# A gated attention/SSM block on one Trainium2 core: the output projection in Strassen's seven products per pair of token tiles, and the SSM gate computed ahead and kept in DRAM

## The chip, the cores and the metric

The kernel runs on one core of a Trainium2 chip. The metric is device time in microseconds (us). TensorE (PE) multiplies matrices, VectorE (DVE), ScalarE (ACT) and GpSimd (POOL) do the element-wise work, SyncE (SP) only issues DMA transfers; ACT issues some too. Each engine works through its own list of instructions in a fixed order and waits where it must: an instruction that waits holds up all that stand behind it on that engine.

## The reference

The sequence has L = 1024 tokens of width D = 1024, one layer, all float32.

```
h = rms_norm(x, norm_gain)
q,k,v,z_a,u,z_s,g_a,g_s = split(h @ w_in)
y_a = (band_attention(q,k,v) * silu(z_a)) @ w_attn_out
y_s = gelu(s5_ssm(u));  a,b = split(y_s @ w_glu + b_glu)
y_s = ((a * sigmoid(b)) * silu(z_s)) @ w_ssm_out
merged = sigmoid(g_a + bias_a) * y_a + sigmoid(g_s + bias_s) * y_s
out = rms_norm(x + merged @ w_out, final_gain)
```

`merged` and `w_out` are both 1024 x 1024.

## The kernel before

PE holds a 128 x 128 block of one operand as weights and streams up to 512 columns of the other past it. Every float32 product is made of three matmuls (`mm3`, lines 104 to 106): an operand is split into a rounded part `hi` (ACT, `split_hi`, line 98) and a remainder `lo` (DVE, `split_lo`, line 101), and hi*hi, hi*lo and lo*hi are added up in a PSUM bank.

Work up to the end of attention (about 463 us) is the same before and after, but for where two pools of tiles lie. What follows is a `Stream` of tasks, one after the other on PE. While a task runs, the weights of the next one are loaded (SP) and, half way through, split (ACT, DVE). Two kinds of tasks matter here:

- projection tasks (`proj_task`): 128 columns of `h @ w_in`, 2 halves x 8 x 3 = 48 matmuls, reading `hT` (the normed input, transposed, in the pool `h16`);
- output tasks (`o_task`): 128 rows of a product with 512 inner columns, 2 halves x 4 x 3 = 24 matmuls.

The order is: the last three g_a projections (`ga[NGA:]`), eight attention output tasks (`a_task`, whose evacuation multiplies by sigmoid(g_a) into the tiles `mg`), the g_s projection 0, eight GLU tasks, the g_s projection 1, and then in turn the SSM output task m (`gs[m][1]`) and the g_s projection m + 2. Here sigmoid(g_s) stays in a tile `sg` until the SSM output task of the same rows needs it. The GLU input is read back from DRAM into tiles `yr` and split into `g_hi` and `g_lo` between the attention output tasks and the GLU tasks. `w_out` is loaded by `load_wo` (512 KB a time, tile `wo_raw`) and split during the last tasks.

The last section (lines 1201 to 1246) takes eight tiles of 128 tokens. For each: load the residual row `x` (512 KB), split the 128 columns of the eight `mg` tiles into `mh` and `ml`, then 2 halves x 8 x 3 matmuls of 512 columns; the last token tile takes its second half as two of 256. `add_x` adds PSUM to `x` (DVE), ACT squares and sums, POOL multiplies by the final gain, and after the second half a chain of small instructions (`rsqrt`) gives 1/rms. The scaled row goes to a tile of its own, `o`, and from there to DRAM: the first half by ACT's queue, the second by SP's. There are two `x` tiles and two `o` tiles, so the next `x` load waits only for a DVE and an ACT instruction.

Of the kernel before, what the change touches and what calls it, by code (L numbers as in the profile page):

```python
# [45 lines left out]
def trunk_kernel(ctx: ExitStack, tc: tile.TileContext, x, x_t, ng, w_m, w_v, bias, a_re, a_im, log_dt,  # L46
# [1039 lines left out]
    def o_task(src, y, evac):  # L1086
# [9 lines left out]
        return (o_dma(src), o_split, run, 2)  # L1096

    def a_task(m, y):
        def evac(half, ps):
# [4 lines left out]
        return o_task(w_ao[m], y, evac)

    def gs_tasks(m, y):
        sgs = {}

        def evac_g(half, ps):
            sgs[half] = rest.tile([P, HALF], F32, tag="sg", name="sg", bufs=6)  # L1110
            act.activation(out=sgs[half], in_=ps, func=AF.Sigmoid, bias=gb[:, KT + m:KT + m + 1])
# [12 lines left out]
    def glu_tasks(m):
        sgs = {}

        def evac_b(half, ps):
# [190 lines left out]
```

## Time and profile before

| | us |
|---|---|
| median of 3 runs (805.6 to 806.41) | 806.41 |
| the profiled execution | 806.33 |
| its span in the trace | 804.5 |
| outside the span (806.33 - 804.5) | 1.8 |
| PE busy | 791.9 (98%) |
| DVE, ACT, POOL busy | 487.9, 361.1, 128.6 |

How to read it: busy times are of one engine each and overlap. PE's instructions are pipelined, so the trace's duration of one matmul is longer than the distance between two; distances are taken from starting times. The groups of instructions give line, engine, operation, out<-in, the number of instructions, busy time, mean duration and what ended the idle time before them.

### The profile page before, as it was taken

To read this page: it belongs to the slowest core of one execution; us is meant where nothing else is said; L and a number is where in the kernel's file an instruction comes from. 1 tells how busy PE (TensorE), PEld (TensorE's weight loads), DVE (VectorE), ACT (ScalarE), POOL (GpSimd) and SP (SyncE) were. 2 spreads that over 40 slices of the span, in tenths; PEclk is the share of its full clock that TensorE was granted. 3 is DMA by queue.
4 is the path that set the end of the run, shared out by engine and by line. 5 is a ranking of instruction groups with operands and counts; after the bars stand their busy time and mean duration, and the time that the engine had idled before them with its cause. 6 is when DMAs were issued, how large, how long until landed. Compare 5 with 4: busy or idle time off the path is not lost.

```text
span 804.5 us, 11004 instructions
## 1 busy us (share of the span) xinstructions
PE 791.9 (98%) x3942; PEld 663.6 (82%) x3942; DVE 487.9 (61%) x1342; ACT 361.1 (45%) x685; POOL 128.6 (16%) x171
## 2 busy tenths in 40 slices
PE   8999999999999999999999999999999999999996
PEld 6778888888887888888888888888888888888885
DVE  6999997978747878787455432344463322454442
ACT  5653456646436566666444582134251111324332
POOL 4560022020202333433122100000000000001111
PEclk9999999999999999999999999999999999999999
DMA  8603433223331011111000262124122110133321
GB/s 315 262 27 105 117 85 116 96 82 132 92 127 44 27 44 43 44 44 43 28 26 27 79 210 65 42 74 135 46 89 88 53 39 1 53 105 105 105 104 54
DMA packets 32455, 67.84 MB, mean 84 GB/s; under 512 B 4560, under 2 KB 13776, under 8 KB 32400
## 3 DMA queue, kind: packets, MB, share of 16 engines
q1 hardware_dynamic: 27904, 61.35, 22.9%
q10 hardware_dynamic: 3344, 3.42, 1.5%
q0 software_dynamic: 1152, 2.36, 1.5%
q8 instruction: 31, 0.51, 0.3%
q14 instruction: 24, 0.20, 0.1%
HBM read 56.14 MB, written 10.98 MB: 83 GB/s over the span
## 4 chain that ended last, share of the span: by engine, by line
PE 89%; DVE 7%; ACT 2%; issue 1%; DMA 1%; POOL 0%; ACTq 0%; DVEq 0%
PE mm L104 25%; PE mm L106 25%; PE mm L105 25%; PE pt L943 2%; PE pv L962 2%; PE s L914 1%; PE pv L961 1%; DVE p L916 1%; PE s L915 1%; DVE tl L101 1%; PE pt L442 1%; PE b L468 1%; PE pt L503 1%; PE pt L504 1%; DVE qq L92 1%
## 5 line engine op out<-in xcount | busy, mean ns | idle before, releaser
L104 PE MATMUL mm<-hT,w_hi 128*128 128x512 f32 x576 | 233.1, 405 | 0.0
L106 PE MATMUL mm<-hT,w_lo 128*128 128x512 f32 x576 | 225.6, 392 | 0.8 <-DVE w_lo L101 0.8
L105 PE MATMUL mm<-hT,w_hi 128*128 128x512 f32 x576 | 225.4, 391 | 0.0
L106 PEld LDWEIGHTS mm<-hT,w_lo 128*128 128x128 f32 x576 | 108.1, 188 | 24.4 <-DVE w_lo L101 1.2
L105 PEld LDWEIGHTS mm<-hT,w_hi 128*128 128x128 f32 x576 | 108.6, 189 | 16.4 <-issue 0.4
L104 PEld LDWEIGHTS mm<-hT,w_hi 128*128 128x128 f32 x576 | 108.4, 188 | 16.2 <-issue 0.2
L101 DVE TENSOR_TENSOR w_lo<-w_raw,w_hi 128x1024 fp32r<-128x1024 f32 x36 | 44.3, 1231 | 66.0 <-ACT w_hi L98 65.8
L98 ACT ACTIVATE w_hi<-w_raw 128x1024 fp32r<-128x1024 f32 x36 | 38.1, 1059 | 61.1 <-PE mm L105 50.6
L83 POOL TENSOR_TENSOR x<-x,fg_b 128x512 f32<-128x512 f32 (+1 forms) x9 | 11.0, 1227 | 319.1 <-ACT o L1223 319.1
L925 POOL TENSOR_SCALAR p<-p,sm 128x640 f32<-128x640 f32 (+2 forms) x64 | 42.5, 667 | 111.2 <-DVE sm L924 80.8
L923 ACT ACTIVATE p<-p,mx 128x640 f32<-128x640 f32 (+2 forms) x64 | 44.4, 694 | 33.3 <-DVE mx L87 16.7
L101 DVE TENSOR_TENSOR tl<-pt,th 128x512 fp32r<-128x512 f32 (+2 forms) x72 | 43.0, 600 | 24.3 <-ACT th L98 23.8
L98 ACT ACTIVATE th<-pt 128x512 fp32r<-128x512 f32 (+2 forms) x72 | 37.6, 523 | 44.3 <-PE pt L943 43.7
L916 DVE CUSTOM_DVE_ANT_0 p<-s,bias 128x320 f32<-128x320 f32 (+2 forms) x96 | 44.2, 485 | 17.1 <-PE s L915 16.6
L106 PE MATMUL mm<-y_hi,o_lo 128*128 128x512 f32 x128 | 49.8, 389 | 0.0
L104 PE MATMUL mm<-y_hi,o_hi 128*128 128x512 f32 x128 | 49.8, 389 | 0.0
L105 PE MATMUL mm<-y_lo,o_hi 128*128 128x512 f32 x128 | 49.8, 389 | 0.0
L98 ACT ACTIVATE o_hi<-o_raw 128x512 fp32r<-128x512 f32 x24 | 15.0, 631 | 71.7 <-PE mm L105 60.3
L943 PE MATMUL pt<-ident,p 128*128 128x128 f32 x240 | 38.1, 273 | 0.0
L962 PE MATMUL pv<-tl,vt 128*128 128x256 f32 x144 | 36.3, 281 | 1.0 <-DVE tl L101 1.0
L83 DVE TENSOR_TENSOR x<-mm,x 128x512 f32<-128x512 f32 (+1 forms) x17 | 11.2, 660 | 41.5 <-PE mm L106 41.5
L961 PE MATMUL pv<-th,vt 128*128 128x256 f32 x144 | 36.2, 272 | 0.2
(231 smaller groups left out, 1528.2 us busy)
## 6 DMA issues: line engine op xcount, KB each, us to landing
w_raw<-in_w_m_dram SPq DMA_DIRECT2D x36, 512.0 KB, 3.4
x<-in_x_dram SPq DMA_DIRECT2D x16, 512.0 KB, 6.1
wo_raw<-in_w_out_dram SPq DMA_DIRECT2D x8, 512.0 KB, 3.2
xt<-in_x_t_dram SPq DMA_DIRECT2D x6, 512.0 KB, 9.6
bias<-in_bias_dram SPq DMA_DIRECT2D x8, 320.0 KB, 2.9
wv_raw<-in_w_v_dram SPq DMA_DIRECT2D x8, 256.0 KB, 5.4
u_dr<-us SPq DMA_DIRECT2D x4, 512.0 KB, 3.7
uu<-u_dr SPq DMA_DIRECT2D x4, 512.0 KB, 4.4
```

What stands on the lines that cost most here:

```text
L83: (eng or vec).tensor_tensor(out=o, in0=a, in1=b, op=op)
L98: act.activation(out=hi, in_=src, func=AF.Copy)
L101: (eng or vec).tensor_tensor(out=lo, in0=src, in1=hi.bitcast(F32), op=SUB)
L104: pe.matmul(ps, lh, rh, start=first, stop=False)
L105: pe.matmul(ps, lh, rl, start=False, stop=False)
L106: pe.matmul(ps, ll, rh, start=False, stop=last)
L916: vec.tensor_tensor_reduce(out=pr[:, c * cw:(c + 1) * cw], in0=ps, in1=bt[:, 640 - w + c * cw:640 - w + (c + 1) * cw], scale=1.0, scalar=- ...
L923: act.activation(out=pr[:, :w], in_=pr[:, :w], func=AF.Exp, bias=mx[:, 0:1], accum_out=sm)
L925: pool.tensor_scalar(out=pr[:, :w], in0=pr[:, :w], scalar1=sm, scalar2=1.0, op0=MUL, op1=MUL)
L943: last_turn[0] = pe.transpose(tp[:, n:n + P], probs[h, q][:, k * P:(k + 1) * P], ident).ins
L961: pe.matmul(o, lhs, th[:, cs], start=first and n == 0, stop=False)
L962: pe.matmul(o, lhs, tl[:, cs], start=False, stop=last and n == len(blocks) - 1)
```

## The change

The output projection now takes two token tiles at a time (128 tokens each, called a pair below, 0 to 3). With `merged` rows and columns cut in two, and `w_out` in two by two blocks B11 to B22, seven products of half size replace eight:

- `prepare_wo` makes T1 to T4, differences of blocks of `w_out` (POOL), and splits B11, B21, B22 and T1 to T4 into tiles `wb`; it is called four times, in the attention output stage, the GLU stage and twice in the SSM output stage.
- `derive` makes S1 to S4, sums and differences of blocks of `merged` (DVE for pair 0, POOL for the rest; two tiles `s`).
- Products are added up in PSUM banks (three for a pair, four for pair 0), and a bank is added to a half row of `x` each time it holds what is wanted there, so that P1 is read three times: 9 additions of 512 columns for a pair (11 for pair 0) where there were 4.
- A row is scaled in place and leaves from its own `x` tile. There are three `x` tiles, for four pairs of two rows.

The order of stages changes too: all eight g_s projections come first, and sigmoid(g_s) goes to DRAM (`sgs_dr`, 16 writes of 256 KB) and is read back by each `so_task`. Then the attention output tasks, the GLU tasks and the SSM output tasks. After the last projection the pools `h16` and `wp` are closed, and the pool `wo` (the `merged` tiles `mgd` and the tiles `wb`, which `g_hi` and `g_lo` use first) takes their place in SBUF. The GLU input is prepared after the first task and a half of the attention output stage.

```diff
-    h16 = ctx.enter_context(tc.tile_pool(name="h16", bufs=4))
-    wp = ctx.enter_context(tc.tile_pool(name="wp", bufs=2))
+
+    h16_cm = tc.tile_pool(name="h16", bufs=4, side="right")
+    h16 = h16_cm.__enter__()
+    wp_cm = tc.tile_pool(name="wp", bufs=2, side="right")
+    wp = wp_cm.__enter__()
...
+    def o_task(src, y, evac, before=None, late=False):
+
         def run(w):
-            yh, yl = y
+            if before is not None:
+                before()
+            pss = [pm(), pm()] if late else [None, None]
+
+            def piece(half, k):
+                mm3(pss[half], w[0][:, k, :], w[1][:, k, :], y[0][k][:, cut(half)], y[1][k][:, cut(half)],
+                    k == 0, k == 3)
+
+            if late:
+                for half in range(2):
+                    for k in range(3):
+                        piece(half, k)
             for half in range(2):
-                ps = pm()
-                sl = slice(half * HALF, (half + 1) * HALF)
-                for k in range(4):
-                    mm3(ps, w[0][:, k, :], w[1][:, k, :], yh[k][:, sl], yl[k][:, sl], k == 0, k == 3)
-                evac(half, ps)
+                if not late:
+                    pss[half] = pm()
+                for k in range(3 if late else 0, 4):
+                    piece(half, k)
+                evac(half, pss[half])
...
+    def gs_task(m):
+        def evac(half, ps):
+            sg = half_tile()
+            act.activation(out=sg, in_=ps, func=AF.Sigmoid, bias=gb[:, KT + m:KT + m + 1])
+            nc.sync.dma_start(out=sgs_dr[m][:, cut(half)], in_=sg)
+        return proj_task(w_m[28 + m], evac)
...
+            tt(merged(m, cut(half)), ps, ga_, MUL)
         return o_task(w_ao[m], y, evac)
 
-    def gs_tasks(m, y):
+    def so_task(m, y):
+        sgs = []
+
+        def before():
+            for half in range(2):
+                sgs.append(half_tile())
+                nc.sync.dma_start(out=sgs[half], in_=sgs_dr[m][:, cut(half)])
+
+        def evac(half, ps):
+            tt(sgs[half], ps, sgs[half], MUL)
+            tt(merged(m, cut(half)), merged(m, cut(half)), sgs[half], ADD)
+        return o_task(w_so[m], y, evac, before, m == 0)
...
-    seq = ga[NGA:] + [a_task(m, ya) for m in range(KT)] + [gs[0][0]]
-    tail = [gs[1][0]]
-    for m in range(KT):
-        tail.append(gs[m][1])
-        if m + 2 < KT:
-            tail.append(gs[m + 2][0])
...
+    gen = stream.run(ga[NGA:] + [gs_task(m) for m in range(KT)], a_all[0])
...
+    wp_cm.__exit__(None, None, None)
+    h16_cm.__exit__(None, None, None)
+    wo_cm = tc.tile_pool(name="wo", reuse_waits="tile", side="right", bufs=14)
+    wo = wo_cm.__enter__()
+    mgd.extend(wo.tile([P, 4, L], F32, tag=f"mgd{q}", name="mgd", bufs=1) for q in range(2))
...
+    def load_rows_wo(j):
+        raws = []
+        for q in range(2):
+            r = rest.tile([P, D], F32, tag="yr", name="wo_raw")
+            nc.sync.dma_start(out=r, in_=w_out[(j + 4 * q) * P:(j + 4 * q + 1) * P, :])
+            raws.append(r)
...
+        b11, b12 = raws[0][:, cut(0)], raws[0][:, cut(1)]
+        b21, b22 = raws[1][:, cut(0)], raws[1][:, cut(1)]
+        t3 = half_tile()
+        tt(t3, b22, b12, SUB, pool)
+        t2 = half_tile()
+        tt(t2, t3, b11, ADD, pool)
+        keep("B11", b11)
+        keep("T3", t3)
+        keep("T2", t2)
+        t4 = half_tile()
+        tt(t4, b21, t2, SUB, pool)
+        t1 = half_tile()
+        tt(t1, b12, b11, SUB, pool)
+        keep("B21", b21)
+        keep("B22", b22)
+        keep("T1", t1)
+        keep("T4", t4)
...
+    for n, _ in enumerate(stream.run(a_all, glu[0])):
+        if n == 2:
+            ygr = []
+            for b in range(4):
+                yr = rest.tile([P, T8, NJ], F32, tag="yr", name="yr")
+                nc.sync.dma_start(out=yr, in_=y_dr[b].rearrange("t p j -> p t j"))
+                src = yr.rearrange("c t j -> c j t")
+                hi = wo.tile([P, L], F32R, tag="wb", name="g_hi")
+                lo = wo.tile([P, L], F32R, tag="wb", name="g_lo")
+                v3 = "c (j t) -> c j t"
+                split_hi(hi.rearrange(v3, t=T8), src)
+                split_lo(lo.rearrange(v3, t=T8), src, hi.rearrange(v3, t=T8))
+                yg[0].append(hi)
+                yg[1].append(lo)
+            prepare_wo(0, load_rows_wo(0))
...
+    for n, _ in enumerate(stream.run(glu, so_all[0])):
+        if n == 3:
+            prepare_wo(1, load_rows_wo(1))
...
+    for n, _ in enumerate(stream.run(so_all)):
+        if n in (1, 5):
+            j = 2 + n // 5
+            prepare_wo(j, load_rows_wo(j))
...
-            for k, n in order:
-                mm3(pss[n], mh[:, k, :], ml[:, k, :], wo_h[k][:, cols[n]], wo_l[k][:, cols[n]], k == 0, k == KT - 1)
-                if k == KT - 1:
-                    add_x(n, pss[n])
...
+    MATES = {"P1": ("A11", "B11"), "P2": ("A12", "B21"), "P3": ("S4", "B22"), "P4": ("A22", "T4"),
+             "P5": ("S1", "T1"), "P6": ("S2", "T2"), "P7": ("S3", "T3")}
+    ORDER = [("P1", "a", (1, 2, 3)), ("P6", "b", (1,)), ("P5", "c", (3,)), ("P7", "b", (3,)),
+             ("P3", "c", (1,)), ("P4", "b", (2,)), ("P2", "a", (0,))]
+    FIRST = [("P1", "a", (1, 2, 3)), ("P7", "d", (2, 3)), ("P6", "b", (1, 3)), ("P5", "c", (3,)),
+             ("P4", "b", (2,)), ("P3", "c", (1,)), ("P2", "a", (0,))]
...
+        xi = []
+        for r in range(2):
+            xi.append(fin.tile([P, D], F32, tag="x", name="x", bufs=3))
+            nc.sync.dma_start(out=xi[r], in_=x[tok[r], :])
...
+        eng = vec if first else pool
+
+        def derive(name, p, q, op):
+            t = fin.tile([P, HALF], F32, tag="s", name="s")
+            blk[name] = t.rearrange("p (k m) -> p k m", m=P)
+            tt(blk[name], blk[p], blk[q], op, eng)
...
+            inv = rsqrt(fin, ss[r][:, 3:4])
+            for k, col in reversed(list(enumerate(rows[r]))):
+                v = xi[r][:, col]
+                if k == len(rows[r]) - 1:
+                    stt(v, v, inv, fg_b[:, col], MUL, MUL)
+                elif k == 0:
+                    act.activation(out=v, in_=v, func=AF.Copy, scale=inv)
                 else:
+                    ts(v, v, inv, MUL)
+                (nc.scalar if k == 0 else nc.sync).dma_start(out=out[tok[r], col], in_=v)
...
+        DER = {"S3": [("S3", "A11", "A21", SUB)], "S2": [("S1", "A21", "A22", ADD), ("S2", "S1", "A11", SUB)],
+               "S4": [("S4", "A12", "S2", SUB)]}
...
+            two = last and pn == "P2"
+            cuts = [slice(0, HALF)] if not two else [slice(0, HALF // 2), slice(HALF // 2, HALF)]
+            for cs in cuts:
+                for k in range(4):
+                    w = wb[bn, k]
+                    o, h, l = pss[bk][:, cs], w[:, 0, cs], w[:, 1, cs]
+                    pe.matmul(o, a[:, 0, k, :], h, start=new and k == 0, stop=False, skip_group_check=True)
+                    pe.matmul(o, a[:, 0, k, :], l, start=False, stop=False, skip_group_check=True)
+                    pe.matmul(o, a[:, 1, k, :], h, start=False, stop=k == 3, skip_group_check=True)
+                for b in to:
+                    col = slice((b % 2) * HALF + cs.start, (b % 2) * HALF + cs.stop)
+                    v = xi[b // 2][:, col]
+                    tt(v, pss[bk][:, cs], v, ADD)
+                    if b in ends:
+                        r = b // 2
+                        other = b ^ 1
+                        complete(b, cs, parts[other] <= 0 and cs.stop == HALF)
```

In the order of SP's instructions, the end of the program before reads as follows (`x_...` are residual rows, one to a token tile; `o_...` the scaled rows):

```order
L1208 DMA x_6788<-in_x_dram 128x1024
L1208 DMA x_6878<-in_x_dram 128x1024
L1246 DMA out_0_dram<-o_6808 128x512
L1208 DMA x_6968<-in_x_dram 128x1024
L1246 DMA out_0_dram<-o_6898 128x512
L1208 DMA x_7058<-in_x_dram 128x1024
```

And after the change, where x_6942 and x_6944 are the rows of pair 0, x_7111 and x_7113 of pair 1, x_7278 and x_7280 of pair 2, x_7445 and x_7447 of pair 3:

```order
L1291 DMA x_7111<-in_x_dram 128x1024
L1335 DMA out_0_dram<-x_6944 128x512
L1291 DMA x_7113<-in_x_dram 128x1024
L1335 DMA out_0_dram<-x_6942 128x512
L1291 DMA x_7278<-in_x_dram 128x1024
L1335 DMA out_0_dram<-x_7113 128x512
L1335 DMA out_0_dram<-x_7111 128x512
L1291 DMA x_7280<-in_x_dram 128x1024
L1291 DMA x_7445<-in_x_dram 128x1024
L1335 DMA out_0_dram<-x_7280 128x512
L1335 DMA out_0_dram<-x_7278 128x512
L1291 DMA x_7447<-in_x_dram 128x1024
```

Before, a load follows an output that leaves from another tile; now x_7113, x_7280 and x_7447 each take the tile of the row that leaves just ahead of them, in this order x_6944, x_7113, x_7280, and wait for both halves of that row to have reached DRAM.

DVE at the beginning of the attention output stage, before the change (`mg_4387` is the first merged tile, `mm` a PSUM bank):

```order
L83 TENSOR_TENSOR mg_4387<-mm_5356,mg_4387 128x512
L83 TENSOR_TENSOR mg_4387<-mm_5375,mg_4387 128x512
L101 TENSOR_TENSOR o_lo_5408<-o_raw_5390,o_hi_5407 128x512
L83 TENSOR_TENSOR mg_4553<-mm_5392,mg_4553 128x512
L83 TENSOR_TENSOR mg_4553<-mm_5411,mg_4553 128x512
```

and after it:

```order
L103 TENSOR_TENSOR g_lo_5925<-yr_5922,g_hi_5924 128x1024
L85 TENSOR_TENSOR mgd_5863<-mm_5867,mg_4387 128x512
L103 TENSOR_TENSOR g_lo_5931<-yr_5928,g_hi_5930 128x1024
L85 TENSOR_TENSOR mgd_5863<-mm_5886,mg_4387 128x512
L103 TENSOR_TENSOR o_lo_5919<-o_raw_5901,o_hi_5918 128x512
L103 TENSOR_TENSOR g_lo_5937<-yr_5934,g_hi_5936 128x1024
L85 TENSOR_TENSOR mgd_5863<-mm_5903,mg_4553 128x512
L103 TENSOR_TENSOR g_lo_5943<-yr_5940,g_hi_5942 128x1024
L85 TENSOR_TENSOR mgd_5863<-mm_5979,mg_4553 128x512
L103 TENSOR_TENSOR o_lo_6012<-o_raw_5994,o_hi_6011 128x512
L103 TENSOR_TENSOR wb_5954<-wo_raw_5946,wb_5954 128x512
```

The four `g_lo` now stand one ahead of each of the first four evacuations of PSUM, and the splits of `w_out` follow. ACT's order has the four `g_hi`, then wb_5954, wb_5957, wb_5960, wb_5967, wb_5970, and only then `o_hi_6047`, the weights of the fifth attention output task (numbered a4 below, from a0).

DVE at the beginning of the last section, before the change: six of the eight splits of the first token tile (`ml_6791`) stand ahead of, and among, the last SSM output tasks.

```order
L101 TENSOR_TENSOR ml_6791<-mg_5079,mh_6790 128x128
L83 TENSOR_TENSOR sg_6491<-mm_6622,sg_6491 128x512
L83 TENSOR_TENSOR mg_5204<-mg_5204,sg_6491 128x512
L101 TENSOR_TENSOR ml_6791<-mg_5204,mh_6790 128x128
L83 TENSOR_TENSOR sg_6522<-mm_6641,sg_6522 128x512
```

After the change, where sg_6903 is the second half of the last SSM output task, s_6966 is S3, s_6986 is S1, a11_6939 is the split of A11 and a_6968 that of S3:

```order
L85 TENSOR_TENSOR sg_6903<-mm_6920,sg_6903 128x512
L85 TENSOR_TENSOR mgd_5864<-mgd_5864,sg_6903 128x512
L85 TENSOR_TENSOR s_6966<-mgd_5863 128x512
L85 TENSOR_TENSOR s_6986<-mgd_5863,mgd_5864 128x512
L103 TENSOR_TENSOR a11_6939<-mgd_5863,a11_6939 128x512
L103 TENSOR_TENSOR a_6968<-s_6966,a_6968 128x512
```

The split of the first product's operand, which needs only the first four merged rows, now stands behind the last evacuation, S3 and S1. On PE, the last pair's products stand as P1(3) and P7(2) (the number of the pair in brackets), P6(3), P5(3), P2(2), P3(2), P4(2), P7(3), then P2(3) in 256 columns, P3(3), P4(3), and P2(3) in the other 256.

More of the change, by code (lines that the diff above doesn't have):

```diff
@@ L1059, in trunk_kernel, with half_tile, cut, split_tiles @@
     rest = rest_cm.__enter__()
-    def split_y(raws):
+    sgs_dr = [dr.tile([P, L], F32, name=f"sgs_dr{m}") for m in range(KT)]
+    def half_tile():
+        return rest.tile([P, HALF], F32, tag="sg", name="sg", bufs=5)
+    def cut(half):
+        return slice(half * HALF, (half + 1) * HALF)
+    def split_tiles(raws, pool_, tag, name):
         hs, ls = [], []
         for r in raws:
-            hi = vp.tile([P, L], F32R, tag="v", name="y_hi")
-            lo = vp.tile([P, L], F32R, tag="v", name="y_lo")
+            hi = pool_.tile([P, L], F32R, tag=tag, name=name + "_hi")
+            lo = pool_.tile([P, L], F32R, tag=tag, name=name + "_lo")
             split_hi(hi, r)
@@ L1157, in trunk_kernel @@
         pass
-    for b in range(4):
-        yr = rest.tile([P, T8, NJ], F32, tag="yr", name="yr")
-        nc.sync.dma_start(out=yr, in_=y_dr[b].rearrange("t p j -> p t j"))
-        src = yr.rearrange("c t j -> c j t")
-        hi = vp.tile([P, L], F32R, tag="v", name="g_hi")
-        lo = vp.tile([P, L], F32R, tag="v", name="g_lo")
-        v3 = "c (j t) -> c j t"
-        split_hi(hi.rearrange(v3, t=T8), src)
-        split_lo(lo.rearrange(v3, t=T8), src, hi.rearrange(v3, t=T8))
-        yg[0].append(hi)
-        yg[1].append(lo)
@@ L1169, in trunk_kernel @@
[L1169 to L1171 removed]
+    wp_cm.__exit__(None, None, None)
[3 more added lines that the diff above has]
+    mgd.extend(wo.tile([P, 4, L], F32, tag=f"mgd{q}", name="mgd", bufs=1) for q in range(2))
+    SPOTS = [(wo, "wb")] * 6 + [None] * 10 + [(wo, "wb")] * 8 + [(zp, "z")] * 4
+    for n in range(10):
+        SPOTS[6 + n] = (qk_pools[n // 5], "blk")
@@ L1172, in trunk_kernel @@
+    for n, _ in enumerate(stream.run(glu, so_all[0])):
+        if n == 3:
+            prepare_wo(1, load_rows_wo(1))
+    hs, ls = split_tiles(zs, vp, "v", "y")
     ys[0].extend(hs)
     ys[1].extend(ls)
-    wo_h, wo_l = [None] * KT, [None] * KT
-    big = []
-    def load_wo(k):
-        raw = rest.tile([P, D], F32, tag="yr", name="wo_raw")
-        nc.sync.dma_start(out=raw, in_=w_out[k * P:(k + 1) * P, :])
-        if k < 2:
-            hi, lo = (zp.tile([P, D], F32R, tag="z", name="wo_z") for _ in range(2))
-        elif k < 3:
-            hi, lo = (qk_pools[1].tile([P, D], F32R, tag="blk", name="wo_b") for _ in range(2))
-        else:
-            if not big:
-                big.extend(h16.tile([P, 4, D], F32R, tag="h16", name="wo_h") for _ in range(4))
-            j = k - 3
-            hi, lo = big[j // 4][:, j % 4, :], big[2 + j // 4][:, j % 4, :]
-        split_hi(hi, raw)
-        split_lo(lo, raw, hi)
-        wo_h[k], wo_l[k] = hi, lo
@@ new lines, in trunk_kernel @@
+    FIRST = [("P1", "a", (1, 2, 3)), ("P7", "d", (2, 3)), ("P6", "b", (1, 3)), ("P5", "c", (3,)),
+             ("P4", "b", (2,)), ("P3", "c", (1,)), ("P2", "a", (0,))]
+    fin_cm = tc.tile_pool(name="fin", reuse_waits="tile", bufs=2)
+    fin = fin_cm.__enter__()
+    a11 = fin.tile([P, 2, 4, P], F32R, name="a11", bufs=1)
+    fg_b = fin.tile([P, D], F32, name="fg_b", bufs=1)
+    nc.scalar.dma_start(out=fg_b, in_=fg.partition_broadcast(P))
+    banks = [(ps_m, "mm")] * 3 + [(ps_2, "s")] * 2 + [(ps_t, "pt")] * 2
```

140 lines of the change are left out of this document (72 added, 68 removed).

## The prediction

> **What bounds the kernel now.** I read the page first: busy times, then the chain that ended last.
>
> ```profile
> PE 791.9 (98%) x3942; PEld 663.6 (82%) x3942; DVE 487.9 (61%) x1342; ACT 361.1 (45%) x685; POOL 128.6 (16%) x171
> PE 89%; DVE 7%; ACT 2%; issue 1%; DMA 1%; POOL 0%; ACTq 0%; DVEq 0%
> ```
>
> PE is busy nearly always and carries the chain. Whether that holds where the change is made is told by the windows (busy time of each engine, then the granted clock):
>
> ```profile
> 458.00:700.00 242.00, 242.00 (x1073) 200.43 (x1072) 88.91 (x114) 76.10 (x106) 1.29 (x1) 1.00 0.23 72
> 700.00:780.00 80.00, 80.00 (x355) 66.24 (x354) 39.64 (x124) 30.45 (x98) 7.73 (x6) 1.00 0.31 106
> ```
>
> From the end of attention on PE never idles, at full clock; DVE has half of its time free, ACT more. So a matmul taken away is worth its full distance to the next, and any wait of PE that appears is a loss at its full length. The distances are in the timeline (start, duration), from the last token tile:
>
> ```profile
> 790.62 0.39 PE L104 MATMUL mm<-wo_h,mh 128*128 128x512 f32 x1
> 790.85 0.39 PE L105 MATMUL mm<-wo_h,mh 128*128 128x512 f32 x1
> 791.98 0.28 PE L104 MATMUL mm<-wo_z,mh 128*128 128x256 f32 x1
> 792.10 0.28 PE L105 MATMUL mm<-wo_z,mh 128*128 128x256 f32 x1
> 797.61 0.28 PE L106 MATMUL mm<-wo_h,ml 128*128 128x256 f32 x1
> ```
>
> One of 512 columns takes 0.227 us (791.98 - 790.62 = 1.36 for six), one of 256 takes 0.12; the 0.39 and 0.28 overlap the next ones. The last one gives way at 797.73.
>
> **What is removed: -11.0.** Before, 8 x 48 = 384 matmuls: 360 of 512 columns and 48 of 256 in the last token tile. After, 4 pairs x 7 products x 4 x 3 = 336: 324 of 512 and 24 of 256. That is 36 x 0.227 + 24 x 0.12 = 11.0 us. All else on PE is the same in number and only moves. The rest of this text asks which waits appear.
>
> **Attention output stage: +3.6.** The durations:
>
> ```profile
> L101 DVE TENSOR_TENSOR g_lo<-yr,g_hi 128x1024 fp32r<-128x1024 f32 x4 | 8.1, 2036 | 5.5 <-ACT g_hi L98 5.5
> L98 ACT ACTIVATE g_hi<-yr 128x1024 fp32r<-128x1024 f32 x4 | 8.1, 2058 | 7.0 <-DMA yr<-y_dr 4.2 <-PE mm L105 2.8
> L98 ACT ACTIVATE o_hi<-o_raw 128x512 fp32r<-128x512 f32 x24 | 15.0, 631 | 71.7 <-PE mm L105 60.3 <-issue 11.4
> L83 DVE TENSOR_TENSOR mg<-mm,mg 128x512 f32<-128x512 f32 x16 | 11.1, 691 | 24.8 <-PE mm L106 24.8
> L1111 ACT ACTIVATE sg<-mm,gb 128x512 f32<-128x512 f32 x16 | 10.9, 680 | 30.1 <-PE mm L106 30.0
> L83 POOL TENSOR_TENSOR x<-x,fg_b 128x512 f32<-128x512 f32 x8 | 10.3, 1289 | 318.0 <-ACT o L1223 318.0
> DMA to landing us min/median/max: 4.1/5.7/8.2
> wo_raw<-in_w_out_dram SPq DMA_DIRECT2D x3, 512.0 KB, 3.3
> ```
>
> The row "to landing" is that of the tile yr. `g_hi` now lies in a pool that takes the place of hT, so it cannot start before the last projection has been evacuated. Let 0 be the end of that projection. ACT ends its sigmoid at 0.9 (0.26 from PE's end to another engine's start, as below in the tail, and 0.68), the first two `g_hi` at 3.0 and 5.05. DVE ends the first `g_lo` at 5.05, and only then evacuates a0's first half, which PE ended at 2.7; second `g_lo` 7.8. The third yr load waits for the first `g_lo` (its tile) and lands at 5.1 + 4.1 = 9.2, the fourth at 12.0. So `g_lo` three ends at 13.4 and four, behind an evacuation, at 16.2. The w_out loads take the same two tiles: they land at 16.9 and 19.7. POOL makes T3 and T2 by 21.2 and 22.5; ACT, in order, splits T3, T2, B21 and B22 by 24.5 and comes to a4's weights at 24.5 to 25.2; DVE gives their lo part at 26.0. PE wanted a4 at 8 x 2.72 = 21.8; its first half ends at 28.05 instead of 24.5. Of the stall some 1 us is in two earlier waits, for banks that DVE evacuates late at 14.1 and 16.9; nothing makes it up, since PE is the bound. Bounds: 2 (if yr's loads overlap more) to 6 (with the median 5.7 for both). I take 3.6.
>
> **GLU to SSM output: +1.2.** No wait in the GLU stage: its evacuations are alone on DVE. At the first SSM output task, `late=True` puts 18 matmuls ahead of those which need the last input part, and these hide its split; but on DVE a w_out split, whose load waits for POOL to be done with the tile, stands ahead of the first evacuation. By the same rows that is 1.2 late (0 to 2.5). The 16 sigmoid tiles go out and come back in 256 KB pieces, as the o tiles do below (2.6 to 2.9 us), over a task of 5.4 us or more: 0.
>
> **Start of the last section: +2.9.** Let 0 be the end of the last SSM output task. DVE has two operations of its evacuation (0.26 to 1.64), S3 (2.33), S1 (3.0), and then the lo part of A11 (3.7). PE can do two matmuls of P1, which need only hi, and a few of P7, and waits for 3.7: of 3.7 some 0.8 is worked. Before, the first token tile's splits stood ahead among the last tasks, and PE had no wait there (the window 700:780). Bounds 2.0 and 3.7, by how many matmuls PE does meanwhile.
>
> **The x tiles: +2.75 and +10.1.** The rows from the DMA view of 690 to 806, and the tail:
>
> ```profile
> x<-in_x_dram SPq DMA_DIRECT2D x8, 512.0 KB, 4.0
> out_dram<-o ACTq DMA_DIRECT2D x8, 256.0 KB, 2.9
> out_dram<-o SPq DMA_DIRECT2D x7, 256.0 KB, 2.6
> 797.93 0.42 DVE L83 TENSOR_TENSOR x<-mm,x 128x256 f32<-128x256 f32 x1 [1.71 <-PE mm L106]
> 798.39 0.42 ACT L1223 ACTIVATE o<-x 128x256 f32<-128x256 f32 x1 [2.36 <-DVE x L83]
> 798.93 0.16 DVE L92 SCALAR_TENSOR_TENSOR ss<-ss 128x1 f32<-128x1 f32 x1 [0.57 <-ACT o L1223]
> 800.20 0.49 DVE L92 SCALAR_TENSOR_TENSOR o<-x,rs_r,fg_b 128x256 f32<-128x256 f32 x1
> 800.26 0.72 ACT L1243 ACTIVATE o<-x,rs_r 128x512 f32<-128x512 f32 x1 [0.73 <-DVE rs_r L83]
> 801.01 0.34 ACTq L1246 DMA_DIRECT2D out_dram<-o  x1
> ```
>
> From the last matmul to a scaled row takes 800.98 - 797.73 = 3.25 for 256 columns, and 0.5 more for 512 (0.69 for 0.42 in the addition, 0.63 for 0.42 in the square). Then a tile that takes a row's place must wait out the row's trip to DRAM, 2.9, and its own load, 4.0. Before, a load followed an addition and a scaling, without the 2.9, a whole token tile (10.9 us) ahead.
>
> Pair 3's second row, x_7447, takes the tile of x_7280. With t from the start of the section: P4(2), which completes x_7280, ends when PE has done 288 matmuls and the two waits before it, 288 x 0.227 + 2.9 + 2.75 = 70.95. Its row is scaled at 70.95 + 3.75 = 74.7, and about 0.6 later since x_7278's chain stands between (three small instructions): 75.3. Out by 78.2, loaded by 82.25, two additions of P1(3) by 83.7. PE has P7(3) left to hide it (12 x 0.227 = 2.7) and then P2(3), which needs the bank that holds P1(3): it is free at 73.65 and waits 10.1. Behind this wait stand only P2, P3 and P4, 8.3 us, then the tail, so nothing comes back. Bounds 8 to 12: 3.2 to 4.8 for the load, 1.9 to 4.0 for the output, which are the smallest and largest of these rows.
>
> Pair 0 to 1 is the same chain with more cover (x_7113 in the tile of x_6944), but it begins late. Pair 0 gives DVE 11 additions, four derived blocks and their splits, at 0.69 each, in an order in which the last addition to x_6944 comes at 24.1, though P4(0) ends at 20.4 (77 matmuls and 2.9). Then ACT's square, a table load, and more:
>
> ```profile
> L114 ACT ACT_TABLE_LOAD x1 | 1.3, 1283 | 0.0
> ```
>
> Two splits and two squares stand between on ACT (0.63 to 0.8 each), the row's copy ends at 29.2 and its output is issued at 30.7, behind one more split. 30.7 + 2.9 + 4.0 = 37.6, two additions by 39.1; P2(1), which needs that bank, was due after 148 matmuls, 148 x 0.227 + 2.9 = 36.4: 2.75 (0.9 to 4.5 by the same extremes). Pair 1 to 2: some 1 us of slack, 0.
>
> **The clock: +1.7.** After such an idle stretch the granted clock is a question. This profile has one, at the start:
>
> ```profile
> 6.10:9.50 3.40, 2.04 (x6) 0.81 (x4) 1.13 (x3) 1.61 (x4) 1.44 (x1) 1.00 0.89 265
> 9.50:13.00 3.50, 3.49 (x9) 2.48 (x10) 3.50 (x4) 2.07 (x4) 2.77 (x2) 0.55 1.04 389
> 11.25 0.63 PE L105 MATMUL mm<-wv_lo,hT 128*128 128x512 f32 x1
> 11.68 0.63 PE L106 MATMUL mm<-wv_hi,hT 128*128 128x512 f32 x1
> ```
>
> Where PE was busy for 2.0 of 3.4 us, the next 3.5 ran at 0.55, with 0.43 between matmuls instead of 0.227. Ten idle microseconds should do as much: half of 3.4 us lost, 1.7, in the 8.3 that are left (0 to 3.4). For the waits of 1 to 4 us I take nothing: one stretch of 1.4 idle is all that this profile has, and how often a shorter one costs clock is a rival below.
>
> [...]
>
> **The tail: +1.65.** Both rows of the last pair end together: their two chains interleave on DVE and ACT, and the last copy (0.72) stands behind the other row's. With 0.9 for five small instructions of the other row on DVE and ACT (0.16 to 0.2 each, as 798.93) that is 1.65 beyond the 801.01 - 797.73 = 3.3 of before. Bounds 1 and 2.2.
>
> **Sum.** -11.0 + 3.6 + 1.2 + 2.9 + 2.75 + 10.1 + 1.7 + 1.65 = +12.9, on the profiled execution of 806.33 (the median of the runs is 806.41): 819.2. All low ends give 809, all high ends 830.
>
> **Rivals.**
> - **All waits hidden, faster.** The decisive mechanism is the last x tile: were its output and load done within P7(3) (2.7 us where they need 10 to 13), and DVE's order no obstacle, only the matmuls and the tail would count: 806.33 - 11.0 + 1.65 = 797. For it: DVE and ACT have half their time free. Against: the wait is a chain of latencies, not of load. 0.06.
> - **The early waits are absorbed.** The banks give PE work across 1 to 3 us, and the a stage, the GLU edge and pair 0 to 1 show little: 819.2 - 3.6 - 1.2 - 2.75 = 811.7. Against: PE executes in order, and the waits are for weights, not only banks. 0.24.
> - **Each wait halves the clock.** By the row of 6.10 to 9.50, three more windows of 1.7: 824.3. 0.17.
> - **The change doesn't do what it says**: more matmuls than counted. The order of PE's instructions has the 336; under 0.01.
>
> **How the numbers follow.** The forecast of 819 (815 to 822) has 0.52, the rivals as above. The range 810 to 826 takes in the forecast, the absorbed case and most of the clock case; it leaves the faster case and the ends of the bounds. Runs of this kernel can tell 0.2% (1.6 us) from no change. Slower: 0.9; the same: 0.04; faster: 0.06.
>
> **What would show it.** Right: a gap of 8 to 12 us on PE before P2 of the last pair, ended by DVE's addition to x, and this by a DMA of x; in the last 12 us a granted clock near 0.5 to 0.8; a gap of 2 to 4 at the first P1; gaps in the attention output stage ended by the fifth task's o_hi or o_lo. Wrong: PE idle under 2 us before that P2, which would mean that the row leaves earlier or that the load needs less than these rows say; or a stage that I call free (g_s projections, GLU) with PE waiting for SP's longer list.

## The result, and the profile after

The kernel after takes 826.88 us (median of 4 runs, 825.76 to 828.44) against 806.41 beside it on the same chip: ratio 1.0252, 95% interval 1.0228 to 1.0276. It is slower, by more than the forecast of 819.2, and lies 0.9 above the upper end of the range. The profiled execution took 827.12 with a span of 825.3.

The page after (busy times, the granted clock in 40 slices of the span, the chain by engine, one group):

```profile
PE 793.7 (96%) x3882; PEld 658.2 (80%) x3882; DVE 525.9 (64%) x1352; ACT 370.2 (45%) x669; POOL 169.2 (20%) x199
PEclk9999999999999999999999999999989999999997
PE 83%; DVE 8%; DMA 3%; ACT 3%; issue 2%; POOL 1%; ACTq 0%; DVEq 0%; POOLq 0%; SPq 0%
L1358 PE MATMUL c<-wb,a 128*128 128x512 f32 (+1 forms) x116 | 46.6, 403 | 11.5 <-DVE x L85 9.0
```

116 on each of three lines are the 348 matmuls that the forecast counted, 324 of 512 columns and 24 of 256. PE's share fell from 98 to 96 per cent and its chain share from 89 to 83: what the products saved went into waits, 11.5 us of them at the first matmul line of the last section alone. PE is busy 1.8 us longer than before with fewer matmuls, since some of them ran slowly: the dips of the clock row are stretches at half clock.

The waits themselves, in PE's timeline (start, duration, in brackets the idle time ahead and its releaser), each with the row ahead of it:

```profile
602.91 0.39 PE L108 MATMUL mm<-y_hi,o_lo 128*128 128x512 f32 x1
604.92 0.50 PE L106 MATMUL mm<-y_hi,o_hi 128*128 128x512 f32 x1 [1.62 <-DVE wb L103]
605.27 0.39 PE L107 MATMUL mm<-y_lo,o_hi 128*128 128x512 f32 x1
607.83 0.80 PE L108 MATMUL mm<-y_hi,o_lo 128*128 128x512 f32 x1 [2.17 <-DVE o_lo L103]
...
685.20 0.40 PE L108 MATMUL mm<-y_hi,o_lo 128*128 128x512 f32 x1
687.54 0.50 PE L106 MATMUL mm<-y_hi,o_hi 128*128 128x512 f32 x1 [1.94 <-DVE sg L85]
...
722.83 0.39 PE L108 MATMUL mm<-y_hi,o_lo 128*128 128x512 f32 x1
725.79 0.50 PE L1358 MATMUL c<-wb,a 128*128 128x512 f32 x1 [2.57 <-ACT a L100]
...
796.81 0.39 PE L1360 MATMUL c<-wb,a 128*128 128x512 f32 x1
806.15 0.55 PE L1358 MATMUL c<-wb,a 128*128 128x256 f32 x1 [8.96 <-DVE x L85]
```

What a wait costs is the difference of the two starts less 0.227: 1.78 and 2.33 at a4 (the fifth attention output task), 2.11 behind the first SSM output task, 2.73 at the first P1, and 9.11 at P2 of the last pair. The granted clock fell behind three of the four places (windows: length, busy time of PE, PEld, DVE, ACT, POOL, clock, DMA):

```profile
608.50:612.00 3.50, 3.50 (x10) 2.73 (x9) 2.88 (x5) 1.15 (x2) 0.00 (x0) 0.50 0.69 221
688.00:692.00 4.00, 4.00 (x20) 3.26 (x18) 4.00 (x8) 1.44 (x3) 0.83 (x1) 1.00 0.42 115
727.00:730.00 3.00, 3.00 (x8) 2.30 (x7) 2.21 (x5) 1.67 (x3) 0.00 (x0) 0.50 0.89 330
806.20:812.30 6.10, 6.10 (x21) 5.38 (x22) 1.80 (x4) 0.72 (x2) 1.28 (x1) 0.53 0.00 0
```

At clock 0.50 the matmuls of 512 columns stand 0.43 apart here (608.42 to 608.85). Adding up what each distance exceeds the normal one, stretch by stretch, gives this account of 827.12 - 806.33 = +20.8:

| term | forecast | measured |
|---|---|---|
| matmuls removed | -11.0 | -11.0 |
| start to end of attention (same instructions) | 0 | +1.2 |
| attention output stage: waits (with small ones of under 0.4) | +3.6 | +4.8 |
| half clock behind them | 0 | +2.6 |
| GLU to SSM output | +1.2 | +2.5 |
| start of the last section | +2.9 | +2.7 |
| half clock behind it | 0 | +1.6 |
| pair 0 to 1, x tile | +2.75 | 0 |
| last pair, x tile | +10.1 | +9.1 |
| half clock behind it | +1.7 | +2.4 |
| matmuls further apart at full clock | 0 | +3.0 |
| tail | +1.65 | +1.3 |
| sum | +12.9 | +20.2 |

Some 0.6 stays unassigned. For the 1.2 up to the end of attention I can name no part of the change: in the run x4 below the last matmuls of attention stand 1.2 earlier than in the kernel after, where they stand before the change. In the eleven traces with the change the first attention output task begins between 579.8 us (x4) and 581.0 (after), though nothing ahead of it differs but a small tile in pad64; so this term looks like scatter between executions.

### The profile page after: what moved, and what is told of

It reads as the page before. It is cut to its first block, busy times and chain, and to the rows that moved or that the text cites. A ratio compares the mean times of both kernels' runs of the same rounds, so it can differ in the third digit from the quotient of the medians.

```text
span 825.3 us, 11041 instructions
## 1 busy us (share of the span) xinstructions
PE 793.7 (96%) x3882; PEld 658.2 (80%) x3882; DVE 525.9 (64%) x1352; ACT 370.2 (45%) x669; POOL 169.2 (20%) x199
## 4 chain that ended last, share of the span: by engine, by line
PE 83%; DVE 8%; DMA 3%; ACT 3%; issue 2%; POOL 1%; ACTq 0%; DVEq 0%; POOLq 0%; SPq 0%
PE mm L108 20%; PE mm L106 20%; PE mm L107 20%; PE c L1358 3%; PE c L1359 3%; PE c L1360 3%; PE pt L945 2%; PE pv L964 2%; PE s L916 1%; PE pv L963 1%; DVE p L918 1%; PE s L917 1%; DVE tl L103 1%; PE pt L444 1%; PE b L470 1%
## 5 line engine op out<-in xcount | busy, mean ns | idle before, releaser
L1358 PE MATMUL c<-wb,a 128*128 128x512 f32 (+1 forms) x116 | 46.6, 403 | 11.5 <-DVE x L85 9.0
L85 POOL TENSOR_TENSOR sg<-wo_raw 128x512 f32<-128x512 f32 x8 | 12.6, 1572 | 199.3 <-DMA wo_raw<-in_w_out_dram 138.3
L1359 PE MATMUL c<-wb,a 128*128 128x512 f32 (+1 forms) x116 | 46.6, 401 | 0.0
L1360 PE MATMUL c<-wb,a 128*128 128x512 f32 (+1 forms) x116 | 45.6, 400 | 0.0
L85 DVE TENSOR_TENSOR x<-c,x 128x512 f32<-128x512 f32 (+1 forms) x39 | 25.5, 673 | 20.6 <-DMA x<-in_x_dram 10.3
```

Source lines behind the costliest of these rows:

```text
L85: (eng or vec).tensor_tensor(out=o, in0=a, in1=b, op=op)
L1358: pe.matmul(o, a[:, 0, k, :], h, start=new and k == 0, stop=False, skip_group_check=True)
L1359: pe.matmul(o, a[:, 0, k, :], l, start=False, stop=False, skip_group_check=True)
L1360: pe.matmul(o, a[:, 1, k, :], h, start=False, stop=k == 3, skip_group_check=True)
```

## The experiments

All times are medians; the kernel before, on the same chip each time, was 806.44 to 806.49 (806.41 beside the kernel after). "After" is 826.88.

**x4: a fourth x tile.** To make room, the tile that takes the squares is single.

```diff
-            xi.append(fin.tile([P, D], F32, tag="x", name="x", bufs=3))
+            xi.append(fin.tile([P, D], F32, tag="x", name="x", bufs=4))
-            sq = fin.tile([P, HALF], F32, tag="sq", name="sq")
+            sq = fin.tile([P, HALF], F32, tag="sq", name="sq", bufs=1)
```

> Edit: the changed kernel with four x tiles instead of three (one scratch tile for the squares instead of two makes room). Theory: the wait of 9.3 us ahead of P2 of the last pair is the trip of the row x of pair 2 to DRAM and the load of the next row into its tile; with a fourth tile the load is long done, the wait goes, and so does the half clock after it (2.5 us): 826.9 - 9.3 - 2.5 = about 815, with P2 of the last pair starting within 1 us of the end of P7. Rival: DVE's additions and the row's chain hold P2 up as well; then a wait of 3 us or more stays there, ended by DVE and not by a DMA, and the time is 819 or more.

Measured 816.08 (814.14 to 816.85), ratio 1.0116 [1.0101, 1.0131]: 10.8 less than after. In its windows PE does not stop before the last P2:

```profile
787.00:797.00 10.00, 10.00 (x51) 8.36 (x50) 6.07 (x18) 3.08 (x8) 0.00 (x0) 1.00 0.28 107
```

The row that leaves from its own tile, with one tile too few, is shown as the cause of the largest term, with the slow matmuls behind it. The two come to 11.5 and the gain is 10.8; half clock came and stayed away at other waits too (last section below), so the two numbers need not agree.

**wo_late: the first preparation of w_out written later**, in the program behind the fifth attention output task instead of the second one's first half.

```diff
+        if n == 9:
             prepare_wo(0, load_rows_wo(0))
```

> Edit: the changed kernel with the first preparation of w_out moved from the 3rd to the 10th half task of the attention output stage; the GLU input's splits stay where they are. Theory: of the 4.9 us of waits in that stage most come from the splits of w_out that stand ahead of a4's weights on ACT; moved, 1 us or less of waits stays (banks evacuated late behind g_lo), no half clock (2.65 us before): 826.9 - 4 - 2.65 = about 820. Rival 1: the g_hi/g_lo chain with its two loads is the cause: the waits stay over 3 us, time 824 or more. Rival 2: the stall moves with the w_out splits to a later task: the same 4 us of waits, some 11 us later in the stage, time about 827.

Measured 826.29 (824.01 to 831.1), ratio 1.0254 [1.022, 1.0288]. The scheduler put DVE's instructions in the same order as before the edit, and ACT's up to that place, so the waits stayed (the second of the two is shown), and the run tells nothing for or against the theory:

```profile
607.83 0.80 PE L108 MATMUL mm<-y_hi,o_lo 128*128 128x512 f32 x1 [2.17 <-DVE o_lo L103]
```

**wo_late2: the same, with the order forced.** The splits of that preparation may be issued only behind a5's weights on ACT and the evacuation of a4's second half on DVE (`pin` holds these two instructions).

```diff
-            split_hi(t[:, 0, :], src)
-            split_lo(t[:, 1, :], src, t[:, 0, :])
+            with ExitStack() as es:
+                for p in pin:
+                    es.enter_context(tc.issue_after(p))
+                split_hi(t[:, 0, :], src)
+                split_lo(t[:, 1, :], src, t[:, 0, :])
...
-            prepare_wo(0, load_rows_wo(0))
+        if n == 9:
+            prepare_wo(0, load_rows_wo(0), (a_ev[-1], last_hi[0]))
```

> Edit: the changed kernel with the splits of the first preparation of w_out held behind the weights of a5 on ACT and the second half of a4 on DVE (its loads and differences stay early). The run before this one (wo_late) moved the code but not a single instruction on DVE, and its traces show the same two waits at the same place, so it told nothing. Theory: of the 4.9 us of waits in the attention output stage nearly all come from these splits standing ahead of a4's weights on ACT and DVE: 1 us or less stays, and no half clock behind it (2.6 us): 826.9 - 4 - 2.6 = about 820. Rival: the g_hi/g_lo chain with its two loads is the cause: over 3 us of waits stay there, ended by evacuations behind g_lo, time 824 or more.

Measured 819.81 (817.9 to 822.03), ratio 1.0164 [1.0143, 1.0184]: 7.1 less than after. The stretch in which the kernel after has PE busy for 46.20 of 50 us at clock 0.93 is full:

```profile
600.00:650.00 50.00, 50.00 (x219) 40.74 (x218) 30.22 (x43) 18.07 (x30) 11.14 (x8) 1.00 0.31 94
```

So the term is order, not load: the same splits, later in the same engines' lists, leave no wait of over 0.3 us there.

**a11_first: the start of the last section.** S3 and S1 of pair 0 are issued behind A11's split, and the load of the final gain goes from ACT's queue to SP's, behind the first x loads.

```diff
-    nc.scalar.dma_start(out=fg_b, in_=fg.partition_broadcast(P))
+        if first:
+            nc.sync.dma_start(out=fg_b, in_=fg.partition_broadcast(P))
...
+            if first and name == "S3":
+                with tc.issue_after(a11_lo[0]):
+                    tt(blk[name], blk[p], blk[q], op, eng)
```

> Edit: the changed kernel with the load of the final gain moved from ACT's queue to SP's (behind the first two x rows), and S3 and S1 of pair 0 issued behind the split of A11 on DVE. Theory: at the start of the last section PE then has two matmuls at once and waits for the split of A11 until 2.3 us after the last SSM task instead of 3.7: the wait falls from 3.1 to 1.8 us. If a wait of under 2 us costs no clock, the 1.4 us of half clock behind it goes too: 826.9 - 1.3 - 1.4 = about 824. Rival, from the early row of the profile of before where 1.4 us of idle was followed by half clock: the half clock stays, 825.6. Rival 2: the order of DVE does not matter since PE waits on something else: 826.9.

Measured 825.59 (824.46 to 826.46), ratio 1.0233 [1.0216, 1.025]. PE now does two matmuls of P1 and then waits 1.81 instead of 2.73, with no slow matmuls behind:

```profile
724.73 0.40 PE L1370 MATMUL c<-wb,a 128*128 128x512 f32 x1
726.77 0.50 PE L1371 MATMUL c<-wb,a 128*128 128x512 f32 x1 [1.65 <-DVE a L1314]
```

The median moved by 1.3, and the two ranges overlap (the kernel after has 825.76 to 828.44). In the profiled executions these two would give 2.5; but in this one the wait at the first SSM output task was 2.56 and cost 1.6 of clock, which it did not in the kernel after. So the time lies where the rival had it, 825.6, but not for the rival's reason: no half clock stayed behind this wait.

**keep_warm: 30 matmuls ahead of the last P2**, into a spare bank that nobody reads (called dummies here), so that PE is not idle while it waits.

```diff
+            if two:
+                spare = bank()
+                for _ in range(30):
+                    pe.matmul(spare, a[:, 0, 0, :], wb[bn, 0][:, 0, :], start=True, stop=True)
```

> Edit: the changed kernel with 30 matmuls of 512 columns into a spare bank, whose result nobody reads, ahead of P2 of the last pair: 6.8 us of work inside the wait of 9.3 us. Theory: the wait is set by the load of x and stays as it is, but PE is not idle for a whole stretch of 3.4 us, so the matmuls behind it run at full clock: 826.9 - 2.5 = about 824.4, P2's first matmul at the same distance from P4 of pair 2 as before. Rival: the half clock does not come from idling, and the matmuls behind the wait stay at 0.43 us: 826.9.

Measured 827.25 (825.96 to 827.86), ratio 1.0256 [1.0241, 1.0271]: no gain. P2 still waits for the same addition, 2.80 behind the last dummy (807.21 - 804.18 - 0.227). It begins at full clock, where the kernel after has 0.21 between matmuls of 256 columns, but from 1.5 us later the matmuls of 512 columns stand 0.43 apart, until 812.15:

```profile
807.21 0.39 PE L1362 MATMUL c<-wb,a 128*128 128x256 f32 x1 [2.63 <-DVE x L85]
807.43 0.28 PE L1363 MATMUL c<-wb,a 128*128 128x256 f32 x1
...
808.78 0.63 PE L1362 MATMUL c<-wb,a 128*128 128x512 f32 x1
809.21 0.63 PE L1363 MATMUL c<-wb,a 128*128 128x512 f32 x1
```

From this P2 to the last matmul it is 817.13 - 807.21 = 9.92, in the kernel after 817.12 - 806.15 = 10.97: 1.05 is gained, and half clock worth 1.6 us stays, behind a wait of which the dummies leave 2.80 unfilled. This P2 begins 1.06 later here (807.21 for 806.15), which takes the gain away. Of that, 0.70 is the edit's own: three of the dummies ran ahead of P3 and P4 of pair 2 (789.08 to 789.78), so that the row whose tile P2 waits for was completed later; the other 0.36 came along from the stages before. So with all but 2.80 us of the wait filled P2 began at full clock, and half clock came all the same, for a shorter time; that dummies which fill the whole wait would gain time is not shown.

**so_pinned and so_j3: the w_out splits among the SSM output tasks.** so_pinned forces the third and fourth preparation behind the tasks' own instructions, as in wo_late2; so_j3 the fourth alone.

```diff
-            prepare_wo(j, load_rows_wo(j))
+            prepare_wo(j, load_rows_wo(j), (a_ev[-1], last_hi[0]))
```

> Edit: the changed kernel with the splits of the last two preparations of w_out held behind the evacuations and weights of the SSM output task they are called from. Theory: the wait of 2.1 us (2.0 to 2.6 in five runs) behind the first SSM output task comes from a w_out split standing ahead of its evacuation on DVE; it goes: 826.9 - 2.1 = about 824.8, and another 1.4 less in executions in which it costs half clock. Rival: seven splits in a row ahead of the next evacuations give the same wait one or two tasks later: about 827.

> Edit: the changed kernel with only the last of the four preparations of w_out held behind the third SSM output task (so_pinned held the last two, and its wait behind the first SSM task grew from 2.1 to 3.3 us, now behind the splits of the third preparation). Theory: the wait of 2.1 us behind the first SSM output task is the one split of the last preparation that stands ahead of its evacuation on DVE and waits for its load; it goes, 0.5 us or less stays there, and no new wait of over 0.5 us comes behind the third task: 826.9 - 2.1 = about 824.8. Rival: the splits of the third preparation, which stay ahead of the evacuation, hold it up just as long, since POOL is late with their differences: the wait stays at 1.5 us or more, or comes one task later, 826.5 or more.

so_pinned: 830.06 (828.53 to 830.74), ratio 1.0293 [1.0275, 1.031], worse than after and than both figures expected. The splits now stand together ahead of an evacuation (DVE's timeline, then PE's):

```profile
687.94 1.28 DVE L105 TENSOR_TENSOR wb<-sg,wb 128x512 fp32r<-128x512 f32 x2
...
690.35 1.28 DVE L105 TENSOR_TENSOR wb<-sg,wb 128x512 fp32r<-128x512 f32 x2
...
692.16 0.68 DVE L85 TENSOR_TENSOR sg<-mm,sg 128x512 f32<-128x512 f32 x1
...
692.89 0.50 PE L108 MATMUL mm<-y_hi,o_hi 128*128 128x512 f32 x1 [3.15 <-DVE sg L85]
707.26 0.50 PE L108 MATMUL mm<-y_hi,o_hi 128*128 128x512 f32 x1 [1.60 <-DVE sg L85]
```

so_j3: 824.04 (823.08 to 825.43), ratio 1.0216 [1.0197, 1.0236], 2.8 less than after; the wait at the first SSM output task is gone:

```profile
650.00:700.00 50.00, 49.87 (x215) 39.94 (x214) 36.00 (x47) 18.36 (x30) 11.45 (x8) 1.00 0.34 106
```

**pad64: everything on the right-hand side of SBUF 64 bytes further in**, against the matmuls' wider distance.

```diff
+    padr = ctx.enter_context(tc.tile_pool(name="padr", bufs=1, side="right"))
+    padt = padr.tile([P, 16], F32, name="padt")
+    vec.memset(padt, 0.0)
```

> Edit: the changed kernel with a tile of 64 bytes that nobody uses at the right end of SBUF, so that all tiles of that side (hT, then g_hi, g_lo, merged and wb) lie 64 bytes lower; before, left tiles begin 32 bytes and right tiles 96 bytes past a multiple of 128. In the changed kernel matmuls stand 0.233 us apart in the GLU stage and 0.232 in the last section, 0.227 elsewhere, some 2.9 us in all. Theory: this comes from streamed operand (right) and weights (left) lying differently to a multiple of 128 bytes; aligned alike, all stand 0.227 apart and the time is 826.9 - 2.9 = about 824. Rival: it hangs on which tiles lie where, not on 64 bytes; the distances stay, 826.9.

Measured 827.17 (825.37 to 828.06), ratio 1.0251 [1.0236, 1.0266]; the mean distances did not change, so this shift is no remedy.

**all_four and all_four2: the repairs together.** all_four has x4, wo_late2, so_pinned and a11_first; all_four2 has so_j3 in so_pinned's place.

> Edit: four x tiles, both w_out edits (as in wo_late2 and so_pinned) and the A11 edit (a11_first) together, no padding. Theory: the waits are independent and in series on PE, so the gains add: 826.9 - 11.8 (x tiles, with its half clock) - 4 - 2.6 (attention output stage) - 2.1 (first SSM task) - 1.3 (start of the last section) = 805, and 1.4 less where the start costs no half clock: 803.5 to 805.5, no slower than the kernel before at 806.4, by less than 0.4%. Rival: a wait taken away lets the next one grow (pair 0 to 1, forecast at 2.75 and not seen, becomes visible when the start is earlier): 807 to 809.

> Edit: four x tiles, the first w_out preparation held back (wo_late2), only the last one held back (so_j3), and the A11 edit (a11_first) together. all_four came to 813.5 with waits of 3.3 and 2.5 us in the SSM output stage that its pinning of the third preparation made; without that: 813.5 - 5.8 and, where those waits cost half clock there, 1.0 less: 806.5 to 808. From the other side: the matmuls taken out are worth 11.0; what stays is 2.9 (wider distances), 1.3 (tail), 1.8 to 2.3 (start) and 1.4 for half clock behind it where it falls into one window of the clock: 806.4 - 11.0 + 7.4 = 802.8. Theory: between these, 802 to 807, no slower than before. Rival: a new wait in the SSM stage, 809 or more.

all_four: 813.5 (810.17 to 814.89), ratio 1.0078 [1.0053, 1.0104], a miss: so_pinned's waits came along, 3.32 and 2.5. Half clock followed the first of them and the wait at the first P1, 2.33 here. all_four2: **803.65** (9 runs, 802.68 to 805.32) against 806.49 (13 runs), ratio **0.9965, interval 0.9953 to 0.9977**. It beats both kernels, the one before by 0.35%: none of its 9 runs is as slow as the fastest of the 13 (805.71). Its page, and the one wait of more than 0.4 us left on PE from the end of attention to the last matmul:

```profile
PE 785.9 (98%) x3882; PEld 651.7 (81%) x3882; DVE 525.4 (66%) x1352; ACT 369.8 (46%) x669; POOL 169.8 (21%) x199
...
716.14 0.50 PE L1379 MATMUL c<-wb,a 128*128 128x512 f32 x1 [1.64 <-DVE a L1322]
```

The four repairs alone gave 10.8 + 7.1 + 2.8 + 1.3 = 22.0, together 23.2. The 11.0 saved comes out as 2.7 on the profiled executions: 0.8 is start, 2.1 are waits of over 0.3, 1.2 shorter ones, 3.0 the wider distance, 1.4 the tail.

## Why the prediction fell short

**The sign, and the places.** Slower was right, and each gap that it named stands in the trace but one. The largest, forecast at 10.1 by a row's way to DRAM and the load behind it, is 9.1 and released as it said (chain of waits: start, length, what):

```profile
798.17 2.78 DMA out_dram<-x
801.02 3.62 DMA x<-in_x_dram
804.72 1.30 DVE x L85 x2
```

2.78 for 2.9 and 3.62 for 4.0 are half of the missing 1.0.

**The clock, where the forecast failed.** "For the waits of 1 to 4 us I take nothing" is the step. Half clock followed two of those three places, 2.6 and 1.6: 4.2 of the 7.9 by which the forecast was low. Its rival "each wait halves the clock" had counted 5.1 for three windows and would have given 824.3; which of the waits lose clock did not go by their length (last section below). I had the row that speaks for it, 2.04 us busy of 3.4 followed by 0.55, and set it aside as a single case. Nor does any run show what keep_warm was expected on, that PE must be idle for a whole stretch of 3.4 us: half clock followed a wait of 2.73 in the kernel after and one of 2.80 in keep_warm. The forecast's 1.7 behind the long wait was an estimate from that one row; measured there are 2.4, with a clock of 0.53 over the 6.1 us from 806.20.

**The attention output stage: mechanism right, size off.** The chain has the steps that the forecast listed, each behind the last:

```profile
583.90 2.05 DVE g_lo L103
585.97 4.02 DMA yr<-y_dr
...
596.78 3.05 DMA wo_raw<-in_w_out_dram
600.00 1.29 POOL sg L85
...
601.97 1.23 DVE wb L103
...
604.81 2.37 DVE wb L103 x2
607.17 0.61 DVE o_lo L103
```

Five splits of w_out stand on DVE between a3's `o_lo` and a4's, four of them in the last 6 us. The waits are 4.8 for 3.6, within the bounds of 2 to 6. The forecast had the lo part of a4's weights 0.8 behind the hi part; here it is 2.9 (604.87 to 607.78). Three of the splits, at 601.97, 603.72 and 604.81, took 1.23, 1.16 and 1.76 us while POOL computed differences of w_out, together 2.1 more than at the 0.69 that they take alone. Of the 28 such splits in this trace six overlapped a POOL operation by more than 1.1 us, and these took 1.16 to 1.78; the others took 0.68 to 0.69. No run separates this part of the wait. The row at 604.92 names DVE as releaser, but ACT's `o_hi`, from 604.26 to 604.87, ends just ahead of it. In wo_late2, with these splits behind, the waits are gone.

**GLU to SSM output: 2.5 for 1.2**, at the upper bound. Behind the split of the last input part, DVE had not one split of w_out ahead of the evacuation but three, and the third waited for ACT; so_j3, in which the fourth preparation comes later, has no such wait:

```profile
683.81 1.28 DVE L103 TENSOR_TENSOR wb<-sg,wb 128x512 fp32r<-128x512 f32 x2
686.19 0.69 DVE L103 TENSOR_TENSOR wb<-wo_raw,wb 128x512 fp32r<-128x512 f32 x1 [1.11 <-ACT wb L100]
686.80 1.28 DVE L85 TENSOR_TENSOR sg<-mm,sg 128x512 f32<-128x512 f32 x2
```

**The start of the last section: 2.7 for 2.9, for another reason.** The forecast had PE do two matmuls of P1 on the hi part and wait for lo. But hi was late too: ACT stood at the load of the final gain, which it issued only when DVE had ended its last evacuation (723.98 + 0.69 = 724.67). The forecast had not counted that load in ACT's list.

```profile
723.98 0.69 DVE L85 TENSOR_TENSOR mgd<-mgd,sg 128x512 f32<-128x512 f32 x1
724.70 0.36 ACTq L1276 DMA_DIRECT2D fg_b<-in_fg_dram  x1
725.11 0.63 ACT L100 ACTIVATE a<-mgd 128x512 fp32r<-128x512 f32 x1 [12.33 <-DVE mgd L85]
```

In a11_first, where S3, S1 and the load are out of the way, PE behaves as the forecast had it. That run changed both at once, so their shares are open.

**Pair 0 to 1: 0 for 2.75.** The chain was there but quicker (SP's queue, then DVE's):

```profile
751.82 0.34 SPq L1335 DMA_DIRECT2D out_dram<-x  x1
754.67 0.33 SPq L1291 DMA_DIRECT2D x<-in_x_dram  x1
...
758.14 1.29 DVE L85 TENSOR_TENSOR x<-c,x 128x512 f32<-128x512 f32 x2 [0.98 <-DMA x<-in_x_dram]
```

Counted from the section's start at 723.06 the row goes out at 28.8 (forecast 30.7) and the two additions end at 36.4 (39.1), while P2(1) was due at about 38.6: later than the forecast's 36.4 by the slow clock at the start and the wider distance. This error of 2.75 happened to cover part of the others.

**Matmuls further apart: +3.0, not foreseen.** "A matmul taken away is worth its full distance" took the distance as fixed. First and last of 46 starting times, 45 distances, in a GLU task after, and the same number before (in projection and SSM output tasks; the GLU tasks of before have 0.2269 as well):

```profile
632.17 0.39 PE L106 MATMUL mm<-g_hi,o_hi 128*128 128x512 f32 x1
642.67 0.39 PE L106 MATMUL mm<-g_hi,o_hi 128*128 128x512 f32 x1
...
632.18 0.39 PE L104 MATMUL mm<-hT,w_hi 128*128 128x512 f32 x1
642.38 0.39 PE L104 MATMUL mm<-hT,w_hi 128*128 128x512 f32 x1
```

10.50 / 45 = 0.2333 us against 10.20 / 45 = 0.2267. It holds for the 192 matmuls of the GLU tasks and, at 0.232, for the last section, in the traces of all the kernels here that have the change. The GLU tasks stream their operand from the pool `wo` on the right-hand side, but in the last section, by `SPOTS` in the code, only 14 of the 28 `wb` tiles lie there. The seven tiles of the second preparation all lie in the pools that held q and k, on the left, and the matmuls that stream them stand 0.231 apart too (27 distances in the kernel after). So the place in `wo` alone does not explain it, and the cause is open; of remedies only the shift of 64 bytes was tried.

**Right as forecast:** 11.0 for the matmuls; nothing for the g_s tiles' way through DRAM; the tail, 1.3 for 1.65. (The 0.26 from PE's end to another engine's start is 0.20 in the tail's rows, 797.93 - 797.73; at the sigmoid ahead of `g_hi` it was 0.25.) "All waits hidden" would have been 797; with the four repairs it is 803.65, held up by what the account of all_four2 lists.

## What to carry to other kernels

Fewer products pay only while PE is fed: here 11 us of matmuls were lost again to the order of instructions on DVE and ACT and to one missing tile, with DVE idle for 36 per cent of the span and ACT for 55. A tile that leaves in place is held for its row's trip to DRAM and the next load, 6.4 us here, so count one buffer more than for a row that is copied out; and put preparation behind the splits and evacuations that PE waits for, engine by engine, since moving it in the program moved nothing. Price a wait of 2 to 3 us with the slow matmuls that may follow it, here 1.1 to 1.6 us.

## What the runs showed of the clock

In the kernel after PE stands for 2.11 us at the first SSM output task and for 2.73 at the first P1. The same two waits, in the traces of the kernels here that have the change and keep the wait, by the clock of the matmuls behind them (0.23 us apart at full clock, 0.43 at half):

| wait | full clock behind it | half clock behind it |
|---|---|---|
| first SSM output task | 2.11 (after), 2.56 (wo_late2) | 2.00 (wo_late), 2.12 (pad64, x4), 2.42 (keep_warm), 2.56 (a11_first), 3.3 (so_pinned, all_four) |
| first P1 | 1.81 (a11_first, all_four2), 2.33 (so_pinned), 2.72 (so_j3), 2.73 (x4, keep_warm, wo_late2) | 2.33 (all_four), 2.72 (wo_late), 2.73 (after, pad64) |

So a wait of the same length may cost clock or not: 2.33, 2.56 and 2.73 stand in both columns. That it hangs on the moment at which a wait falls is my estimate. Where half clock followed one of these waits, it cost 1.1 us (all_four, first SSM output task) to 1.6 (the kernel after, first P1). After the wait at the first P1, in x4:

```profile
722.80:725.80 3.00, 0.46 (x3) 0.04 (x1) 2.47 (x4) 0.65 (x2) 0.00 (x0) 1.00 0.73 236
725.80:730.00 4.20, 4.17 (x18) 3.28 (x19) 3.41 (x7) 2.18 (x4) 0.00 (x0) 1.00 0.99 365
```

Full clock and 18 matmuls in 4.2 us, where the kernel after has 8 in 3.0 at 0.50. So a single repair can move the time by more or less than its own wait: behind waits that it does not touch half clock may come or go, as in a11_first and keep_warm at the first SSM output task.
